# A decoder layer on one core: modulation rows through GpSimd's DMA queue, conditioning row by transposes

## The chip, the core and the metric

One Trainium2 chip, one of its cores. The metric is the device time of one execution in microseconds (us), 1265.94 us as the median of 3 runs of the kernel before (1265.94 to 1266.82). The engines have the profile's names: PE (matmul) with PEld (its weight loads), DVE (vector), ACT (scalar), POOL (GpSimd), SP (which here only issues DMAs). Each engine works through its own instructions in the order in which they stand; semaphores make one wait for another.

## The reference, cut to what matters

One residual layer on x of 256 x 2048 in float32, with a conditioning vector c of 2048:

```
mod = silu(c) @ w_mod + b_mod            # 2048 x 12288, six sections of 2048
sh1, sc1, g1, sh2, sc2, g2 = split(mod, 6)
u = x * (1 + sc1) + sh1
y = token_mixer(u)                       # u @ w_in, then mLSTM heads and HGRN2 heads, then @ w_out
x = layer_norm(alpha * x + (1 + g1) * y)
u = x * (1 + sc2) + sh2
y = (silu(u @ w_gate) * (u @ w_up)) @ w_down     # 5632 wide
x = layer_norm(alpha * x + (1 + g2) * y)
```

HGRN2 has a lower bound `lb`, computed from 8 columns of logits.

## The kernel before, in words

**Modulation.** `w_mod` lies in 96 rows of [128, 2048] floats, 1024 KB each (`in_wmod`). `mod(j)` (line 171) loads row j into a tile `m` of a pool with two buffers (`mr`), and one DVE instruction (L174) multiplies it with `cb` and sums along the row, which gives column j of `modc`. `cb` is silu(c) on all 128 partitions. It is loaded as a broadcast (L140) and put through Silu by ACT. Rows 0 to 15 are the shift and 16 to 31 the scale of the first modulation; they are needed in pairs, one pair for each block k of 128 features (k from 0 to 15). The other 64 rows serve the gate of the first residual, the second modulation and the last gate.

**Activations.** `make_u(k)` (L268) makes block k of u from a slice of `xT` and the pair of columns: one ACT instruction for `t`, one for its rounded part `uh`, one DVE subtraction for the rest, `ul`. `xT` comes in four loads of four blocks each.

**Weights.** All other weights come as tiles of [128, 1024] floats, 512 KB (`wr`, four buffers). ACT rounds each into `wh` (five buffers), DVE subtracts to get the rest `wl` (five buffers, L213 in the first stages and L715 later), and PE runs three matmuls for each product: high by high, low by high, high by low. So each weight tile costs one ACT instruction, one DVE instruction and 24 matmuls of 256 columns or their like.

**Stages.** First stage: the input projection, in an order written in `STAGES`: sections q and f for blocks 0 to 3, then the other sections for blocks 0 to 7, then q and f for blocks 4 to 15. `prep` calls `mod(16+k)`, `mod(k)` and `make_u(k)` for each block as it is due. Then the rest of the projection with the HGRN2 and mLSTM work between its tiles; then the output projection (`wo`) with the mLSTM tail and the first layer norm; then the feed-forward part, nearly two thirds of the time. Further mod rows are called at set rates between tiles (`mods_some`, L610ff.), and the last ones in the feed-forward part (`some` at L787, called at L906, and `up_to`).

**Order.** The order of the code is not the order on the engines. A scheduler walks through the instructions by priority and by when it thinks their inputs and buffers are ready, and fixes one order for each engine. The loads of mod rows and of weight tiles are all issued by SP, in that one order: an issue that waits for a free buffer holds up all that stand behind it. The lower bound's Exp needs another function table on ACT.

Of the kernel before, what the change touches and what calls it, by code (L numbers as in the profile page):

```python
# [3 lines left out]
F32 = mybir.dt.float32  # L4
F32R = mybir.dt.float32r
U8 = mybir.dt.uint8
AF = mybir.ActivationFunctionType
ALU = mybir.AluOpType

P = 128  # L10
# [69 lines left out]
def build(nc, tc, d):  # L80
    from contextlib import ExitStack

    with ExitStack() as ctx:
# [41 lines left out]
        def act(out, in_, f, **kw):  # L125
            if f in sets:
                use_set(f)
            i = nc.scalar.activation(out, in_, f, **kw).ins  # L128
            if f in sets:
                tc.add_manual_dep(i, table["load"].name, order, reason="table")  # L130
                table["used"].append(i)
            return i
# [4 lines left out]
        mm = nc.tensor.matmul  # L137

        cb = cst.tile([P, D], F32, name="cb")
        nc.sync.dma_start(cb, d["c"].broadcast_to([P, D]))  # L140
        pk = cst.tile([P, NPK], F32, name="pk")
        nc.sync.dma_start(pk, d["pk"])
        kc = cst.tile([P, NCST], F32, name="kc")
        kr = cst.tile([P, 256], F32R, name="kr")
        mk = cst.tile([P, NMK], U8, name="mk")

# [10 lines left out]
        one = cst.tile([P, P], F32, name="one1")  # L157
        nc.gpsimd.memset(one, 1.0)

        for i in range(2):  # L160
            o = cb[:, 1024 * i : 1024 * i + 1024]
            act(o, o, AF.Silu)
        init = cst.tile([P, 96], F32, name="init")
        nc.vector.tensor_copy(init, pc("bmod", 0, 96))
        for s in (1, 2, 4, 5):
            ts(init[:, 16 * s : 16 * s + 16], pc("bmod", 16 * s, 16), 1.0, None, ALU.add)
        ca = cst.tile([P, 16], F32, name="ca")
        act(ca, pc("c", 0, 16), AF.Silu)
        modc = cst.tile([P, 96], F32, name="modc")

        def mod(j):
            t = mr.tile([P, D], F32, tag="m", name=f"m{j}")
            nc.sync.dma_start(t, d["wmod"][j])
            table["mod"] = nc.vector.tensor_tensor_reduce(t, t, cb, 1.0, init[:, j : j + 1], ALU.mult, ALU.add, modc[:, j : j + 1]).ins  # L174
            yield

# [92 lines left out]
        def make_u(k):  # L269
            u = S(T, "t", bufs=CFG["t"])  # L270
            if k % 4 == 0:
                xt["t"] = M(name="xT")
                nc.sync.dma_start(xt["t"], d["x"][k // 4])
            act(u, xt["t"][:, (k % 4) * T : (k % 4) * T + T], AF.Identity, scale=col(1, k), bias=col(0, k))
            split(kt(uh, k), kt(ul, k), u)

# [24 lines left out]

        def lower_bound():
            e, pr = lbt[:, 0:8], lbt[:, 8:16]
            tt(e, pc("lb", 0, 8), pc("lb", 0, 8), ALU.subtract)
            act(e, e, AF.Exp)
            nc.vector.reciprocal(pr, e)
            tt(pr, pr, e, ALU.mult)
            tt(lb, pr, pr, ALU.subtract)
            ts(oml, lb, -1.0, 1.0, ALU.mult, ALU.add)
# [14 lines left out]
        def fq_part(k0, k1):  # L324
            banks = [ps() for _ in range(8)]
            for k in range(k0, k1):
                prep(k + 1)
                if k == 3:
                    nc.sync.dma_start(kc, d["kc"])
                    mf = M(NMK, name="mf")  # L330
                    nc.sync.dma_start(mf, d["mk"])
                    nc.vector.tensor_copy(mk, mf)
                    act(kr[:, 0:P], ident, AF.Copy)
                    act(kr[:, P:], kc[:, 192:320], AF.Copy)
                for c, (h, l) in enumerate(next_win()):
                    gB(banks[4 * c : 4 * c + 4], h, l, 1, 1024, uh, ul, k, k == k0, k == k1 - 1)
                    yield
            if k1 == KT:
                next(ga)
            for i in range(8):  # L340
                evac(k0, "fq", i, banks[i])
# [649 lines left out]
def lay(x, c, w_mod, b_mod, w_in, conv_w, conv_b, b_igate, b_fgate, mlstm_norm_w, hgrn_norm_w, lb_logits, w_out, ln1_g, ln1_b, w_gate, w_up, w_down, ln2_g, ln2_b):  # L991
    import numpy as np

    def tile(w, k0, nk, c0, n):
        return w[k0 * P : (k0 + nk) * P, c0 : c0 + n].reshape(nk, P, n).transpose(1, 0, 2).reshape(P, nk * n)

    def cols(v):
        return v.reshape(-1, P).T

    def few(v, at):  # L1000
        return np.concatenate([np.zeros((at, 1), np.float32), v.reshape(-1, 1), np.zeros((P - at - v.size, 1), np.float32)])

    wm, wi, wo, wg, wu, wd = w_mod[0], w_in[0], w_out[0], w_gate[0], w_up[0], w_down[0]
    a = {}
    a["c"] = c.reshape(1, D)
    a["wmod"] = np.ascontiguousarray(wm.T).reshape(96, P, D)
    a["wmk"] = np.concatenate([wm[:, s * D : s * D + D].reshape(KT, P, D) for s in PE_SECT] or [wm[:1, :1].reshape(1, 1, 1)])
    a["x"] = x[0].T.reshape(4, 4, P, T).transpose(0, 2, 1, 3).reshape(4, P, 1024)
    a["pk"] = np.concatenate(
        [cols(b_mod), cols(conv_w), cols(conv_b), cols(mlstm_norm_w), cols(hgrn_norm_w), cols(lb_logits), cols(ln1_g), cols(ln1_b), cols(ln2_g), cols(ln2_b), few(b_igate, 0), few(b_fgate, 32), cols(c)],  # L1010
        axis=1,
    )
    pl = win_plan()
    a["win"] = np.stack([np.concatenate([tile(wi, *p), tile(wi, *q)], axis=1) for p, q in zip(pl[::2], pl[1::2])])
    z = np.zeros((D, 28), np.float32)
    a["wg"] = tile(np.concatenate([wi[:, 3072:3076], z, wi[:, 3076:3080]], axis=1), 0, KT, 0, 36)
    a["wo"] = np.stack([tile(wo, 8 * part + 2 * p, 2, 512 * i, 512) for part in (1, 0) for i in range(4) for p in range(4)])
    a["wf"] = np.stack([np.concatenate([tile(wg, k, 1, 512 * g, 512), tile(wu, k, 1, 512 * g, 512)], axis=1) for g in range(DFF // 512) for k in range(KT)])
    a["wd"] = np.stack([tile(wd, k, 2, 512 * c, 512) for c in range(4) for k in range(0, FB, 2)])
    a["xr"] = x[0].reshape(2, P, D)  # L1020
    for n, v in (("l1g", ln1_g), ("l1b", ln1_b), ("l2g", ln2_g), ("l2b", ln2_b)):
        a[n] = v.reshape(1, D)
    kc = np.zeros((P, NCST), np.float32)
    s = np.arange(P)
    kc[:, 0:128] = np.eye(P)
    kc[:, 128:192] = (s[:, None] % 64) == np.arange(64)[None, :]
    kc[:, 192:320] = np.where(s[:, None] <= s[None, :], 0.0, -1e30)
    a["kc"] = kc
    mk = np.zeros((P, NMK), np.float32)
    for i, cc in enumerate((1, 2, 4, 8, 16, 32)):  # L1030
        ss, t = (s % 64)[:, None], np.arange(64)[None, :]
        mk[:, 64 * i : 64 * i + 64] = (ss // (2 * cc) == t // (2 * cc)) & (ss % (2 * cc) < cc) & (t % (2 * cc) >= cc)
    a["mk"] = mk
    for k in ("win",):
        a[k] = a[k].reshape(-1, P, 2, 1024).transpose(0, 2, 1, 3)
    return {k: np.ascontiguousarray(v) for k, v in a.items()}
# [17 lines left out]
```

## Time and profile before

| | |
|---|---|
| median of the runs | 1265.94 us |
| the profiled execution's own time, and its span | 1265.78 us, 1264.0 us |
| PE / DVE / ACT / POOL busy | 1212.8 / 901.2 / 591.7 / 3.9 us |
| granted TensorE clock, mean | 0.99 of full speed |
| DMA, mean over the span | 260 GB/s |
| mod rows on DVE | 96, 225.1 us busy in total |
| weight tiles on DVE | 408, 360.6 + 135.8 us at the two lines (the page's ACT and DVE rows have them) |

Busy shares are means over stages that differ. The stages below are cut by tiles: at 43 us PE starts on block 3, by 214 us DVE has done 68 weight tiles, by 377 us 111, and the first layer norm's statistics are summed at 508 us. PE's matmuls are pipelined and their ends are modelled, so short waits of PE are seen best as gaps.

### The profile page before, as it was taken

The page shows a single profiled execution, that of the slowest core. Times are in us where ns is not written, and L with a number is a line of the kernel's source. Part 1 is how long each engine was busy: PE and PEld are TensorE (multiplying, and loading weights), DVE is VectorE, ACT ScalarE, POOL GpSimd, SP SyncE. Part 2 cuts the span into 40 slices and gives each one's busy share as a digit, 9 for nine tenths or more (in the row PEclk, how much of TensorE's full clock was granted, in tenths as well). Part 3 has the DMA queues.
Part 4 walks back from the last instruction along what each step waited for, and adds up shares of the span by engine and source line. Part 5 has one row for each costly group of instructions (what it writes and reads, how often), then busy time and mean ns, then how long its engine had stood idle before and what let it go on. Part 6 is the DMA issues. An engine that isn't in the chain of part 4 may idle for free.

```text
span 1264.0 us, 17132 instructions
## 1 busy us (share of the span) xinstructions
PE 1212.8 (96%) x6706; PEld 1040.0 (82%) x6706; DVE 901.2 (71%) x979; ACT 591.7 (47%) x743; POOL 3.9 (0%) x13
## 2 busy tenths in 40 slices
PE   4899999999999999799999999999999999999995
PEld 4888899997889887688888888888888888888884
DVE  6778997999999979997877554455555445445655
ACT  4554454835664644644544444433344444434340
POOL 0000000000000000000000000000000000000000
PEclk9999999999999999899999999999999999999998
DMA  9998997857788989889998666666666666676661
GB/s 364 386 335 328 341 398 285 301 200 264 267 327 308 330 317 334 305 320 327 324 329 325 192 190 189 178 194 191 198 191 192 189 194 185 193 256 184 191 191 66
DMA packets 75968, 328.00 MB, mean 260 GB/s; under 512 B 8432, under 2 KB 8816, under 8 KB 62704
## 3 DMA queue, kind: packets, MB, share of 16 engines
q1 hardware_dynamic: 75888, 326.92, 74.9%
q8 instruction: 52, 0.85, 0.3%
q14 instruction: 28, 0.23, 0.0%
HBM read 324.79 MB, written 2.10 MB: 259 GB/s over the span
## 4 chain that ended last, share of the span: by engine, by line
PE 89%; DVE 5%; ACT 3%; issue 2%; DMA 1%; DVEq 0%; ACTq 0%
PE ps L722 21%; PE ps L725 21%; PE ps L721 21%; PE ps L251 5%; PE ps L249 5%; PE ps L250 5%; PE ps L260 2%; PE ps L261 2%; PE ps L262 2%; DVE m L174 2%; PE ps L447 1%; ACT wh L128 1%; DMA m<-in_wmod 1%; DVE wl L213 1%; PE ps L863 1%
## 5 line engine op out<-in xcount | busy, mean ns | idle before, releaser
L128 ACT ACTIVATE wh<-wr 128x1024 fp32r<-128x1024 f32 x408 | 431.1, 1059 | 550.8 <-PE ps L722 426.2
L715 DVE TENSOR_TENSOR wl<-wr,wh 128x1024 fp32r<-128x1024 f32 x296 | 360.6, 1224 | 283.7 <-ACT wh L128 280.4
L721 PE MATMUL ps<-wh,u2h 128*128 128x512 f32 x704 | 275.6, 392 | 0.3 <-ACT s L128 0.3
L722 PE MATMUL ps<-wh,u2l 128*128 128x512 f32 x704 | 273.7, 389 | 0.1
L174 DVE CUSTOM_DVE_ANT_0 m<-m,cb,init 128x2048 f32<-128x2048 f32 x96 | 225.1, 2346 | 22.3 <-DMA m<-in_wmod 22.0
L725 PE MATMUL ps<-wl,u2h 128*128 128x512 f32 x704 | 217.0, 389 | 0.0
L249 PE MATMUL ps<-uh,wh 128*128 128x256 f32 x640 | 184.4, 292 | 22.5 <-ACT wh L128 17.1
L250 PE MATMUL ps<-ul,wh 128*128 128x256 f32 x640 | 181.8, 286 | 0.0
L251 PE MATMUL ps<-uh,wl 128*128 128x256 f32 x640 | 180.3, 287 | 1.1 <-DVE wl L213 1.0
L721 PEld LDWEIGHTS ps<-wh,u2h 128*128 128x128 f32 x704 | 132.6, 188 | 28.9 <-ACT s L128 0.7
L722 PEld LDWEIGHTS ps<-wh,u2l 128*128 128x128 f32 x704 | 132.0, 188 | 28.0 <-DVE u2l L838 0.8
L725 PEld LDWEIGHTS ps<-wl,u2h 128*128 128x128 f32 x704 | 132.1, 188 | 27.6
L213 DVE TENSOR_TENSOR wl<-wr,wh 128x1024 fp32r<-128x1024 f32 x112 | 135.8, 1221 | 25.1 <-ACT wh L128 24.5
L249 PEld LDWEIGHTS ps<-uh,wh 128*128 128x128 f32 x640 | 123.6, 194 | 25.0 <-ACT wh L128 17.8
L721 PE MATMUL ps<-wh,hid 128*128 128x512 f32 x352 | 137.2, 390 | 0.0
L725 PE MATMUL ps<-wl,hid 128*128 128x512 f32 x352 | 137.0, 389 | 0.0
L722 PE MATMUL ps<-wh,hid 128*128 128x512 f32 x352 | 137.0, 389 | 0.0
L250 PEld LDWEIGHTS ps<-ul,wh 128*128 128x128 f32 x640 | 124.5, 195 | 1.3 <-issue 1.0
L251 PEld LDWEIGHTS ps<-uh,wl 128*128 128x128 f32 x640 | 123.2, 194 | 1.9 <-DVE wl L213 1.8
L725 PEld LDWEIGHTS ps<-wl,hid 128*128 128x128 f32 x352 | 66.1, 188 | 13.9
L721 PEld LDWEIGHTS ps<-wh,hid 128*128 128x128 f32 x352 | 66.1, 188 | 13.6
L722 PEld LDWEIGHTS ps<-wh,hid 128*128 128x128 f32 x352 | 66.1, 188 | 13.6
(179 smaller groups left out, 1017.8 us busy)
## 6 DMA issues: line engine op xcount, KB each, us to landing
m<-in_wmod SPq DMA_DIRECT2D x96, 1024.0 KB, 7.1
wr<-in_wf SPq DMA_DIRECT2D x176, 512.0 KB, 4.2
wr<-in_win SPq DMA_DIRECT2D x112, 512.0 KB, 6.0
wr<-in_wd SPq DMA_DIRECT2D x88, 512.0 KB, 3.6
wr<-in_wo SPq DMA_DIRECT2D x32, 512.0 KB, 5.4
xT<-in_x SPq DMA_DIRECT2D x4, 512.0 KB, 8.0
z<-in_xr SPq DMA_DIRECT2D x2, 1024.0 KB, 8.6
out<-z SPq DMA_DIRECT2D x8, 256.0 KB, 2.4
```

Source lines behind the costliest of these rows:

```text
L128: i = nc.scalar.activation(out, in_, f, **kw).ins
L174: table["mod"] = nc.vector.tensor_tensor_reduce(t, t, cb, 1.0, init[:, j : j + 1], ALU.mult, ALU.add, modc[:, j : j + 1]).ins
L213: tt(l[:, :m], r[:, :m], h[:, :m].bitcast(F32), ALU.subtract)
L249: mm(o, h[:, wsl], kt(uh, k0 + k), start=st, stop=False, skip_group_check=True)
L250: mm(o, h[:, wsl], kt(ul, k0 + k), start=False, stop=False, skip_group_check=True)
L251: mm(o, l[:, wsl], kt(uh, k0 + k), start=False, stop=en, skip_group_check=True)
L260: mm(o, a, h[:, w], start=first and k == 0, stop=False, skip_group_check=True)
L261: mm(o, a, l[:, w], start=False, stop=False, skip_group_check=True)
L715: tt(l, r, h.bitcast(F32), ALU.subtract)
L721: mm(o, a, h[:, w], start=first, stop=False, skip_group_check=True)
L722: mm(o, b, h[:, w], start=False, stop=False, skip_group_check=True)
L725: mm(o, a, l[:, w], start=False, stop=last, skip_group_check=True)
```

## The change

1. `mod(j)` issues its load from GpSimd instead of SP. The 96 loads leave SP's queue and stand in POOL's. The two buffers stay.
2. The broadcast load of c and the two Silu instructions over it are gone. ACT computes silu of the 16 columns of c in `pk`; PE transposes each column, broadcast along 128, into a PSUM bank (16 transposes, 4 banks), and ACT and DVE copy two banks each into `cb`. The identity that transposes need is the first 128 columns of `kc`; they are now loaded near the start, the other 192 later.
3. The first `xT` tile comes in four slices.
4. The remaining constants and the masks (`mf`) are called for at block 5 instead of 3.
5. The lower bound must stand behind a mod instruction on DVE.

```diff
         cb = cst.tile([P, D], F32, name="cb")
-        nc.sync.dma_start(cb, d["c"].broadcast_to([P, D]))
         pk = cst.tile([P, NPK], F32, name="pk")
         nc.sync.dma_start(pk, d["pk"])
         kc = cst.tile([P, NCST], F32, name="kc")
+        nc.sync.dma_start(kc[:, 0:128], d["kc"][:, 0:128])
...
-        for i in range(2):
-            o = cb[:, 1024 * i : 1024 * i + 1024]
-            act(o, o, AF.Silu)
+        ca = cst.tile([P, 16], F32, name="ca")
+        act(ca, pc("c", 0, 16), AF.Silu)
+        for b in range(4):
+            o = ps()
+            for j in range(4):
+                nc.tensor.transpose(o[:, P * j : P * j + P], ca[:, 4 * b + j : 4 * b + j + 1].broadcast_to([P, P]), ident)
+            if b % 2:
+                nc.vector.tensor_copy(cb[:, 512 * b : 512 * b + 512], o)
+            else:
+                act(cb[:, 512 * b : 512 * b + 512], o, AF.Copy)
...
             t = mr.tile([P, D], F32, tag="m", name=f"m{j}")
-            nc.sync.dma_start(t, d["wmod"][j])
+            nc.gpsimd.dma_start(t, d["wmod"][j])
...
                 xt["t"] = M(name="xT")
-                nc.sync.dma_start(xt["t"], d["x"][k // 4])
+                if k:
+                    nc.sync.dma_start(xt["t"], d["x"][k // 4])
+            if k < 4:
+                w = slice(k * T, k * T + T)
+                nc.sync.dma_start(xt["t"][:, w], d["x"][0][:, w])
...
-            tt(e, pc("lb", 0, 8), pc("lb", 0, 8), ALU.subtract)
+            i = tt(e, pc("lb", 0, 8), pc("lb", 0, 8), ALU.subtract).ins
+            tc.add_manual_dep(i, table["mod"].name, order, reason="late")
...
-                if k == 3:
-                    nc.sync.dma_start(kc, d["kc"])
+                if k == 5:
+                    nc.sync.dma_start(kc[:, 128:], d["kc"][:, 128:])
```

The scheduler makes another order of it on every engine. Three places:

DVE at the start, before (`m` is a mod row, `wl` the low part of a weight tile, `ul` that of a block of u, `lbt` the lower bound):

```order
L164 COPY init<-pk 128x96
L304 TENSOR_TENSOR lbt_119<-pk 128x8
L166 TENSOR_SCALAR init<-pk 128x16 x4
L306 RECIPROCAL lbt_119<-lbt_119 128x8
L174 ISA m_128,modc<-m_128,cb,init 128x2048
...
L174 ISA m_131,modc<-m_131,cb,init 128x2048
L174 ISA modc 128x1
L231 TENSOR_TENSOR ul_111<-t_134,uh_109 128x256
L213 TENSOR_TENSOR wl_143<-wr_140,wh_142 128x1024
L213 TENSOR_TENSOR wl_173<-wr_170,wh_172 128x1024
```

The first two mod rows stand behind each other here, with the rest of the lower bound between them.

DVE at the same place now (four banks are copied to `cb` first, two of them by ACT):

```order
L167 COPY cb<-ps_106 128x512
L167 COPY cb<-ps_118 128x512
L179 ISA m_150,modc<-m_150,cb,init 128x2048
L179 ISA modc 128x1
L218 TENSOR_TENSOR wl_165<-wr_162,wh_164 128x1024
L218 TENSOR_TENSOR wl_195<-wr_192,wh_194 128x1024
L218 TENSOR_TENSOR wl_236<-wr_233,wh_235 128x1024
L218 TENSOR_TENSOR wl_266<-wr_263,wh_265 128x1024
L179 ISA m_153,modc<-m_153,cb,init 128x2048
L179 ISA modc 128x1
L218 TENSOR_TENSOR wl_307<-wr_304,wh_306 128x1024
L236 TENSOR_TENSOR ul_133<-t_156,uh_131 128x256
```

The second mod row, which completes the first pair, stood right behind the first; now four weight tiles stand between them.

SP at the start, before (`wr` is a weight tile, 512 KB):

```order
L140 DMA cb<-in_c 128x2048
L142 DMA pk<-in_pk 128x242
L173 DMA m_128<-in_wmod 128x2048
L173 DMA m_131<-in_wmod 128x2048
L273 DMA xT_135<-in_x 128x1024
L208 DMA wr_140<-in_win 128x1024
L208 DMA wr_170<-in_win 128x1024
L173 DMA m_200<-in_wmod 128x2048
L173 DMA m_203<-in_wmod 128x2048
L208 DMA wr_210<-in_win 128x1024
```

Mod rows and weight tiles stand in one queue, two and two.

SP now, its first five issues, and a stretch from the sixteenth on (`wg` are the gate weights):

```order
L141 DMA pk<-in_pk 128x242
L143 DMA kc<-in_kc 128x128
L282 DMA xT_157<-in_x 128x256
L213 DMA wr_162<-in_win 128x1024
L213 DMA wr_192<-in_win 128x1024
...
L213 DMA wr_452<-in_win 128x1024
L279 DMA xT_1105<-in_x 128x1024
L339 DMA kc<-in_kc 128x192
L341 DMA mf_1428<-in_mk 128x384
L279 DMA xT_1657<-in_x 128x1024
L376 DMA wg_2142<-in_wg 128x576
L213 DMA wr_485<-in_win 128x1024
```

SP has no mod row left. Four weight tiles are issued before anything waits, and the later x tiles, constants, masks and gate weights stand ahead of the tenth weight tile; POOL issues the mod rows, each behind the DVE instruction that frees its buffer.

DVE in the output projection, before (`sc` are columns of the second modulation):

```order
L174 ISA m_4723,modc<-m_4723,cb,init 128x2048
L174 ISA modc 128x1
L715 TENSOR_TENSOR wl_4517<-wr_4514,wh_4516 128x1024
L794 TENSOR_TENSOR sc<-pk,modc 128x4
L795 TENSOR_TENSOR sc<-pk,modc 128x4
L796 TENSOR_TENSOR sc<-sc,modc 128x4
L715 TENSOR_TENSOR wl_4538<-wr_4535,wh_4537 128x1024
L715 TENSOR_TENSOR wl_4556<-wr_4553,wh_4555 128x1024
L715 TENSOR_TENSOR wl_4577<-wr_4574,wh_4576 128x1024
L715 TENSOR_TENSOR wl_4595<-wr_4592,wh_4594 128x1024
L715 TENSOR_TENSOR wl_4616<-wr_4613,wh_4615 128x1024
L174 ISA m_4770,modc<-m_4770,cb,init 128x2048
```

One mod row stands for six tiles in this stretch.

DVE in the output projection now, at about the same tile:

```order
L725 TENSOR_TENSOR wl_4522<-wr_4519,wh_4521 128x1024
L179 ISA m_5361,modc<-m_5361,cb,init 128x2048
L179 ISA modc 128x1
L725 TENSOR_TENSOR wl_4542<-wr_4539,wh_4541 128x1024
L725 TENSOR_TENSOR wl_4563<-wr_4560,wh_4562 128x1024
L179 ISA m_5364,modc<-m_5364,cb,init 128x2048
L179 ISA modc 128x1
L725 TENSOR_TENSOR wl_4581<-wr_4578,wh_4580 128x1024
L179 ISA m_5403,modc<-m_5403,cb,init 128x2048
L179 ISA modc 128x1
L725 TENSOR_TENSOR wl_4602<-wr_4599,wh_4601 128x1024
L725 TENSOR_TENSOR wl_4620<-wr_4617,wh_4619 128x1024
```

Mod rows stand closer together here; rows that the code calls for later, in the feed-forward part, stand in this stage now. Counted over the whole of DVE's order, the mod rows that stand ahead of a given place are:

| place in DVE's order | before | now |
|---|---|---|
| ahead of the 7th weight tile | 8 | 5 |
| ahead of the 68th | 32 | 43 |
| ahead of the 111th | 54 | 65 |
| ahead of the first layer norm's BN_AGGR | 70 | 86 |

## Rows read from the trace of the kernel before

**Rows 1.** The page: span, busy us by engine, chain that ended last

```profile
span 1264.0 us, 17132 instructions
...
PE 1212.8 (96%) x6706; PEld 1040.0 (82%) x6706; DVE 901.2 (71%) x979; ACT 591.7 (47%) x743; POOL 3.9 (0%) x13
...
PE 89%; DVE 5%; ACT 3%; issue 2%; DMA 1%; DVEq 0%; ACTq 0%
```

**Rows 2.** Windows by stage: stretch, length, busy us (count) by engine, clock, DMA

```profile
0.00:43.00 43.00, 21.02 (x147) 20.45 (x148) 29.08 (x37) 17.89 (x25) 2.38 (x11) 1.00 0.95 373
43.00:214.00 171.00, 168.05 (x1204) 158.43 (x1203) 143.16 (x142) 87.90 (x112) 1.48 (x2) 0.99 0.90 344
214.00:377.00 163.00, 158.85 (x1392) 142.02 (x1390) 155.69 (x208) 99.34 (x166) 0.00 (x0) 0.99 0.76 272
377.00:507.00 130.00, 127.11 (x666) 108.47 (x664) 116.66 (x138) 64.83 (x83) 0.00 (x0) 1.00 0.90 323
507.00:1264.00 757.00, 737.72 (x3304) 610.59 (x3304) 456.60 (x458) 321.75 (x361) 0.00 (x0) 0.99 0.68 220
```

**Rows 3.** Windows, one stretch of the feed-forward part

```profile
800.00:900.00 100.00, 100.00 (x443) 82.81 (x442) 52.57 (x49) 38.77 (x37) 0.00 (x0) 1.00 0.64 193
```

**Rows 4.** Timeline of PE: start, length, what, count, [idle before <-releaser]

```profile
16.66 0.58 PE L249 MATMUL ps<-uh,wh 128*128 128x256 f32 x1 [16.66 <-ACT wh L128]
...
42.65 0.74 PE L249 MATMUL ps<-uh,wh 128*128 128x256 f32 x4 [3.78 <-ACT uh L128]
...
512.28 3.67 PE L817 MATMUL ps<-kc,z 128*128 128x128 f32 x16 [8.17 <-DVE z L810]
```

**Rows 5.** Timeline of DVE, the mod rows at L174 of the first 40 us

```profile
9.47 2.35 DVE L174 CUSTOM_DVE_ANT_0 m<-m,cb,init 128x2048 f32<-128x2048 f32 x1
...
12.22 2.35 DVE L174 CUSTOM_DVE_ANT_0 m<-m,cb,init 128x2048 f32<-128x2048 f32 x1
...
21.20 2.35 DVE L174 CUSTOM_DVE_ANT_0 m<-m,cb,init 128x2048 f32<-128x2048 f32 x1
...
29.27 2.35 DVE L174 CUSTOM_DVE_ANT_0 m<-m,cb,init 128x2048 f32<-128x2048 f32 x1
...
38.36 2.35 DVE L174 CUSTOM_DVE_ANT_0 m<-m,cb,init 128x2048 f32<-128x2048 f32 x1 [0.20 <-DMA m<-in_wmod]
```

**Rows 6.** Everything on tile m: landing times of its 96 loads

```profile
DMA to landing us min/median/max: 4.8/7.1/9.9
```

**Rows 7.** The chain of waits, first step: start us, us, what

```profile
0.74 4.77 DMA cb<-in_c
```

**Rows 8.** Windows, DMA near full: last come DMA share, GB/s

```profile
3.00:14.00 11.00, 0.00 (x0) 0.00 (x0) 5.32 (x13) 4.88 (x6) 0.00 (x0) 1.00 1.01 408
```

**Rows 9.** DMA issues: KB of one, median us from issue to landing

```profile
pk<-in_pk SPq DMA_DIRECT2D x1, 121.0 KB, 5.1
```

**Rows 10.** The page, costliest groups: rounding and subtraction of a weight tile

```profile
L128 ACT ACTIVATE wh<-wr 128x1024 fp32r<-128x1024 f32 x408 | 431.1, 1059 | 550.8 <-PE ps L722 426.2
...
L213 DVE TENSOR_TENSOR wl<-wr,wh 128x1024 fp32r<-128x1024 f32 x112 | 135.8, 1221 | 25.1 <-ACT wh L128 24.5
```

**Rows 11.** Timeline of ACT: block 0 of u

```profile
14.61 0.60 ACT L128 ACTIVATE t<-xT,modc 128x256 f32<-128x256 f32 x1 [4.16 <-DVE modc L174]
15.24 0.42 ACT L128 ACTIVATE uh<-t 128x256 fp32r<-128x256 f32 x1
```

**Rows 12.** Windows by stage, tile m alone: DVE busy us (mod rows)

```profile
0.00:43.00 43.00, 18.73 (x8) 1.00 0.95 373
43.00:214.00 171.00, 56.32 (x24) 0.99 0.90 344
```

**Rows 13.** Waits of DVE, 43 to 214 us: us in total, times, longest

```profile
DVE wl L213 <- ACT wh L128: 17.9, 20, 2.9
```

**Rows 14.** Waits of SP, the whole span

```profile
SPq L173 <- DVE modc L174: 133.4, 44, 6.0
```

More of the change, by code (lines that the diff above doesn't have):

```diff
@@ L166, in build @@
             ts(init[:, 16 * s : 16 * s + 16], pc("bmod", 16 * s, 16), 1.0, None, ALU.add)
-        ca = cst.tile([P, 16], F32, name="ca")
-        act(ca, pc("c", 0, 16), AF.Silu)
         modc = cst.tile([P, 96], F32, name="modc")
@@ L1004, in lay @@
     a = {}
-    a["c"] = c.reshape(1, D)
     a["wmod"] = np.ascontiguousarray(wm.T).reshape(96, P, D)
```

## The prediction

> **What bounds the kernel now.** I read the page's head first, then the busy time in five stages, then the first 46 us of each engine in order of time, and last the waits of SP and DVE. The page says PE: 1212.8 of 1264.0 us, and 89% of the chain that ended last [rows 1]. The stages say more [rows 2]. In the feed-forward part PE is full in every stretch with DVE half idle [rows 3]. From 43 to 507 us PE is nearly full too (454 of 464 us), but DVE is close behind it: 143.16 of 171, 155.69 of 163, 116.66 of 130 us, 415.5 of 464 in all, and the DMA engines are at a share of 0.90 in the first and last of these. Only in the first 43 us does PE wait for long: it starts at 16.66 us and gets block 3 of u at 42.65 us [rows 4]. So there are two places where a change can move the end: the arrival of the first four blocks, and DVE (or DMA) becoming the limit between 43 and 507 us. What leaves DVE after 507 us is worth nothing.
>
> The first 43 us are a chain of mod rows. The second, fourth, sixth and eighth start on DVE at 12.22, 21.20, 29.27 and 38.36 us [rows 5]; they share one of the two buffers, so each waits for a load that could be issued only when the one before it was done. From the end of the second (12.22 + 2.35 = 14.57) to the end of the eighth (40.71) are three turns of 8.7 us: 2.35 us of DVE and about 6.3 us of issue to landing, a little under the median of 7.1 [rows 6].
>
> **The change part by part.** *Broadcast load, Silu, lower bound.* The load of c took 4.77 us, two Silu 2.00 us [rows 7]. With 1.05 MB (1024 KB) at 408 GB/s [rows 8] taking 2.6 us, 2.2 us of the 4.77 are fixed. In their place come 16 transposes, 3.67 us for the 16 of the trace [rows 4], twice that if the clock is at its lower level then, and two copies behind each other. `pk` now leads the queue: it lands between 3.3 us (0.74 + 2.2 + 0.3) and 5.9 us (its own 5.1, [rows 9]), so `cb` stands between 7.8 and 14 us. The first mod row began at 9.47; it now begins between 9 and 14. This is not what ends the wait, as the next step shows, so I cost it at nothing; at the late end it costs 4 us.
>
> *The second mod row behind four weight tiles.* On DVE four tiles stand between the first and the second mod row now. The fourth must land first. Ahead of it, in whichever order, go two mod rows (2.10 MB), four tiles (2.10), two slices of x, `pk` and the identity (0.45): 4.65 MB, 11.4 us at 408 GB/s. From the first issue at 0.74, with 2.2 us fixed, that is 14.3 us; ACT's rounding 1.06 and DVE's subtraction 1.22 [rows 10] make it 16.6, and the second mod row ends at 19.0 instead of 14.57. After it t and uh (0.60 + 0.42, [rows 11]): PE starts at about 20.1 instead of 16.66.
>
> *The turns.* From there the chain is as before, three turns through one buffer, each a landing and 2.35 us plus 0.05: the eighth mod row ends at 19.0 + 3 x (L + 2.4). In the old queue a mod load had the DMA engines for itself as far as SP's order let it. Now SP issues tiles as their buffers come free, and four x, constant and gate loads of 2.1 MB besides, while POOL issues mod rows, and both run on the same engines. No row shows two queues side by side, so I take L from the shortest, median and longest landing [rows 6]: 4.8, 7.1, 9.9 give 40.6, 47.5 and 55.9 us against 40.71. I take 7.1, the median: the traffic is about that of the busy stretches where it was measured. Then block 3 arrives at 42.65 + 7 = 49.5 us. **First term: +7 us, from 0 to +15.**
>
> The Trainium skill ("DMA: Bandwidth & Descriptors", Issuing engines are not separate DMA queues) says that DMAs issued by different engines run on the same 16 DMA engines and interleave, and that this saves only issue time. The trace agrees as far as one queue can: from 3 to 14 us SP's queue alone has the share at 1.01 [rows 8]. By this rule the second queue brings no bandwidth, and a mod load beside tiles is slower than alone, the upper part of the range.
>
> *Mod rows drawn forward, 43 to 214 us.* By the 68th tile DVE did 8 + 24 mod rows [rows 12]; now 43 stand there, 11 more, 11 x 2.35 = 25.9 us on an engine that had 171 - 143.16 = 27.8 us free in the stage. DMA carries 58.8 MB there at 344 GB/s; 11 rows add 11.5 MB, and what was loaded ahead (about five tiles, three x tiles, the gate weights) takes off 4.5: 65.8 MB, which needs 385 GB/s to fit into 171 us, against 408 at best. Of DVE's free time 17.9 us were waits for ACT's rounded tile [rows 13], which do not go away because DVE has more to do. If all 25.9 us fit into the gaps it costs nothing; if DMA stays at 344 GB/s the stage takes 191 us, +20. Three engines at 98% of one stage do not fit without friction: I take about 40% of the waits that were there, **second term: +8 us, from 0 to +20.**
>
> *214 to 377 us.* 22 mod rows between the 68th and the 111th tile before and now: 0.
>
> *377 to 507 us.* Five more mod rows up to the layer norm (16 before the change, 21 now): 11.8 us on DVE, which was free for 13.3 us [rows 2]. All of it hidden is 0, none is +12. PE has five buffers of tiles to bridge a mod row of 2.35 us, which hides most of one: **third term: +4 us, from 0 to +12.** Around the layer norm the order is one mod row and the same norm steps, so 0.
>
> *After 507 us* DVE is rid of 16 rows, 37.6 us, beside a PE that is full: 0. That is the price of all this: work moves from a place where it was free to one where it is not. *POOL's issues* are off every engine that counts (POOL busy 3.9 us of the span, [rows 1]); what they may cost is a rival below.
>
> **Sum:** 1264.0 + 7 + 8 + 4 = 1283.0 us of span, and 1.8 us around it as now (1265.78), 1284.8; the profiled execution is 0.2 us below the runs' median. Forecast 1285 us. The three ranges together reach from 1266 to 1313.
>
> **The rivals.**
>
> *The extra rows are absorbed.* DVE's gaps before 507 us sum to 13.9 + 27.8 + 7.3 + 13.3 = 62 us [rows 2], and 16 rows need 37.6. If mod rows fill just the gaps that PE's pace leaves, only the start costs: 1266 + 7 = 1273. For it: in the stage up to 214 us DVE's waits came from PE's pace, not its own. Against it: its order is fixed, so a mod row stands between tiles also when a tile is urgent.
>
> *Faster: SP's queue freed.* SP stood 133.4 us before mod loads whose buffer was still in use, 44 times, with tile loads behind them [rows 14]. If that was what made PE wait, the gaps of PE from 43 to 507 us (3.0 + 4.1 + 2.9 = 10 us) go, and if mod loads win against tiles (L at 4.8 or less) the start costs at most 3: 1266 - 7 = 1259. It decides from the point where block 3 arrives by 46 us. Against it: five tiles wait in buffers between SP and PE, and the gaps of PE lie mostly in HGRN2's own steps, which do not wait for loads.
>
> *Mod loads from POOL land late.* A row through one of two buffers has two periods less its own 2.4 us to land. With 35 rows in 171 us the period is 4.9, so 7.4 us are allowed. With a landing of 9 instead of 7.1, DVE waits (9 - 7.4) / 2 for each of 35 rows, 28 us in place of the 8 of the second term less what overlaps, some 16 more, and the start grows by 3 x 1.9: 1285 + 22 = 1307. For it: every mod load now passes an engine whose DMAs this trace does not show, and the median of 7.1 is near the edge already.
>
> The Trainium skill ("SBUF - State Buffer", Who interferes with whom) says that GpSimd writes descriptors through SBUF ports that it shares with DVE, so that some DVE instructions, those in a two-port mode, hold back a DMA issued by GpSimd until they end, and that tensor_tensor did not. No run here shows it yet. If the tile subtractions or the mod rows themselves held it back, each load would come later by up to one of them, 1.22 or 2.35 us, which is this rival.
>
> **How the numbers follow.** Forecast as summed 0.48 (1275 to 1300), absorbed 0.20 (1273), late landings 0.15 (1307), faster 0.12 (1259), and 0.05 that it ends within 0.2% (2.5 us, what a measurement of this kernel can tell from no change). Faster 0.12, same 0.05, slower 0.83. The range from 1264 to 1310 leaves out most of the faster case and the end of the late one.
>
> **What would show it.** Right: the second mod row starts on DVE at 16 to 18 us, behind four tiles; PE starts near 20 and has block 3 near 50 us; DVE is over 97% busy up to the 68th tile, reached 10 to 20 us later; the layer norm's PE gap near 527 us; the feed-forward part as long as before. Wrong in the first term: mod loads land in 5 us beside tiles. Wrong in the second: the 68th tile at 214 + 7. The forecast falls altogether if block 3 comes before 43 us, or if the feed-forward part itself changes in length.

## The result and the profile after: slower by 4.3%

The changed kernel takes 1319.14 us (1316.91 to 1325.78, four runs), the kernel before 1265.94 in the same comparison: ratio 1.043, 95% interval 1.0406 to 1.0455. Forecast were 1285 us and 1264 to 1310. The direction was right, the loss is 53 us and not 19. The profiled execution took 1321.25 us, 2.1 above the median.

From the page of the changed kernel: the span, busy us (share, count) by engine, the chain that ended last by engine.

```profile
span 1319.5 us, 17219 instructions
...
PE 1225.7 (93%) x6722; PEld 1048.7 (79%) x6722; DVE 901.1 (68%) x981; ACT 589.5 (45%) x743; POOL 55.0 (4%) x109
...
PE 62%; issue 22%; DMA 7%; DVE 6%; POOL 2%; ACT 0%; SPq 0%; DVEq 0%; POOLq 0%; ACTq 0%
```

DVE has the same work to 0.1 us [rows 1]. PE's share of the chain falls from 89% to 62%, but much of the chain's "issue" lies beside a PE that is full (from 285.78 to 334.43 us, for one), so the loss is read from stages instead. The stages of [rows 2] can't be compared directly: its cuts at 214 and 377 us are the ends of the 67th and the 109th weight tile, not of the 68th and the 111th, which end at 218.3 and 385.7 us. So here are both kernels, cut at the same places of the program: PE's start on block 3 of u, DVE's end of the 67th and of the 111th weight tile, the first layer norm's statistics. The columns are the stretch, its length, busy us and count of PE, PEld, DVE, ACT and POOL, the granted clock, DMA share and GB/s. The changed kernel:

```profile
0.00:53.39 53.39, 25.68 (x160) 24.86 (x160) 33.80 (x38) 19.86 (x26) 6.14 (x18) 0.78 0.94 358
53.39:246.90 193.51, 172.25 (x1208) 161.19 (x1209) 162.57 (x166) 83.67 (x109) 18.80 (x36) 0.96 0.92 345
246.90:429.40 182.50, 171.17 (x1474) 152.76 (x1472) 163.85 (x220) 106.20 (x174) 14.44 (x26) 0.98 0.72 252
429.40:564.90 135.50, 119.86 (x578) 99.41 (x578) 121.38 (x148) 58.69 (x74) 11.11 (x21) 0.95 0.91 347
564.90:1319.50 754.60, 736.72 (x3304) 610.50 (x3304) 419.46 (x417) 321.08 (x361) 4.47 (x8) 0.99 0.63 196
```

The kernel before:

```profile
0.00:42.65 42.65, 20.67 (x144) 20.10 (x144) 28.73 (x37) 17.54 (x25) 2.38 (x11) 1.00 0.95 373
42.65:214.20 171.55, 168.60 (x1205) 158.97 (x1206) 143.71 (x143) 88.45 (x112) 1.48 (x2) 0.99 0.90 344
214.20:385.70 171.50, 167.35 (x1451) 149.54 (x1450) 164.09 (x218) 104.50 (x173) 0.00 (x0) 0.99 0.76 272
385.70:508.70 123.00, 118.42 (x606) 100.75 (x604) 109.76 (x132) 59.47 (x74) 0.00 (x0) 0.99 0.90 327
508.70:1264.00 755.30, 737.72 (x3304) 610.59 (x3304) 454.90 (x455) 321.75 (x361) 0.00 (x0) 0.99 0.68 220
```

The five stages are longer by 10.7, 22.0, 11.0, 12.5 and -0.7 us, which sums to the 55.5 us of the spans. In the second stage the DMA share and rate are nearly those of before, so it moves 66.8 MB instead of 59.0 at about the same rate. PE idles 42.6 us more in all, and its own busy time is 12.9 us longer (1225.7 for 1212.8) at a mean granted clock of 0.971 for 0.989; no run here parts that from the idle time.

The second stage for tile m alone (columns: DVE, POOL, clock, share, GB/s):

```profile
53.40:246.90 193.50, 82.20 (x35) 18.51 (x35) 0.96 0.92 345
```

So the three stages from block 3 to the norm have 35, 22 and 21 rows in DVE's order, where the kernel before has 24, 22 and 16. In the third stage the count is the same, but the rows are bunched more: 17 of the 22 stand behind at least 91 weight tiles, 14 before. Narrower windows of the changed kernel show it (all engines):

```profile
300.00:340.00 40.00, 40.00 (x420) 33.96 (x420) 39.44 (x63) 24.27 (x44) 0.54 (x1) 1.00 0.48 155
340.00:390.00 50.00, 50.00 (x293) 43.64 (x291) 40.90 (x51) 26.91 (x53) 4.77 (x9) 1.00 0.87 316
390.00:435.00 45.00, 33.55 (x201) 29.10 (x201) 37.64 (x45) 17.50 (x27) 4.22 (x8) 0.86 0.81 293
```

From 300 to 340 us, with two rows, the DMA engines are half idle; of the next 95 us, with 19 rows, PE loses 11.5, all of it behind 390 us. Waits of the changed kernel (us in total, times, longest), DVE's first:

```profile
DVE m L179 <- DMA m<-in_wmod: 62.4, 37, 3.6
DVE wl L218 <- ACT wh L128: 9.9, 10, 2.5
```

```profile
PE ps L254 <- ACT uh L128: 24.4, 4, 16.3
...
PE gps L384 <- DVE q L299: 9.3, 1, 9.3
PE ps L599 <- DVE s L593: 8.0, 1, 8.0
```

Before, DVE waited 24.5 us in these tiles for ACT's rounding [rows 10] and 22.0 us for mod rows; now it waits mostly for mod rows. One way in which that reaches PE stands in DVE's timeline before the 9.3 us wait, which ends at 245.34 us:

```profile
236.30 1.22 DVE L218 TENSOR_TENSOR wl<-wr,wh 128x1024 fp32r<-128x1024 f32 x1
241.09 2.35 DVE L179 CUSTOM_DVE_ANT_0 m<-m,cb,init 128x2048 f32<-128x2048 f32 x1 [3.57 <-DMA m<-in_wmod]
...
243.37 1.22 DVE L218 TENSOR_TENSOR wl<-wr,wh 128x1024 fp32r<-128x1024 f32 x1
244.51 1.28 DVE L299 TENSOR_TENSOR q<-ps,q 128x512 f32<-128x512 f32 x2
```

A row of a later stage waits 3.57 us for its load, and the evacuation of the bank that PE needs (`q`) stands behind it. How much of the loss goes this way is a question for the runs.

### The profile page after: what moved, and what is told of

It reads as the page before. It is cut to its first block, busy times and chain, and to the rows that moved or that the text cites. A ratio compares the mean times of both kernels' runs of the same rounds, so it can differ in the third digit from the quotient of the medians.

```text
span 1319.5 us, 17219 instructions
## 1 busy us (share of the span) xinstructions
PE 1225.7 (93%) x6722; PEld 1048.7 (79%) x6722; DVE 901.1 (68%) x981; ACT 589.5 (45%) x743; POOL 55.0 (4%) x109
## 4 chain that ended last, share of the span: by engine, by line
PE 62%; issue 22%; DMA 7%; DVE 6%; POOL 2%; ACT 0%; SPq 0%; DVEq 0%; POOLq 0%; ACTq 0%
PE ps L731 19%; PE ps L732 19%; PE ps L735 19%; DMA wr<-in_win 3%; DMA m<-in_wmod 2%; POOL m L178 1%; DVE m L179 1%; DVE wl L218 1%; DVE wl L725 1%; PE ps L873 1%; DMA mf<-in_mk 1%; PE ps L254 1%; PE ps L255 1%; PE ps L256 1%; DMA wr<-in_wo 1%
## 5 line engine op out<-in xcount | busy, mean ns | idle before, releaser
L179 DVE CUSTOM_DVE_ANT_0 m<-m,cb,init 128x2048 f32<-128x2048 f32 x96 | 225.2, 2347 | 62.7 <-DMA m<-in_wmod 62.4
L254 PE MATMUL ps<-uh,wh 128*128 128x256 f32 x640 | 187.4, 298 | 29.3 <-ACT uh L128 24.4
L256 PE MATMUL ps<-uh,wl 128*128 128x256 f32 x640 | 185.2, 290 | 4.8 <-DVE wl L218 4.8
L255 PE MATMUL ps<-ul,wh 128*128 128x256 f32 x640 | 185.1, 290 | 0.3 <-DVE ul L236 0.3
L256 PEld LDWEIGHTS ps<-uh,wl 128*128 128x128 f32 x640 | 127.0, 198 | 5.8 <-DVE wl L218 5.8
L255 PEld LDWEIGHTS ps<-ul,wh 128*128 128x128 f32 x640 | 127.4, 199 | 2.2 <-issue 1.2
```

The source lines that it names most:

```text
L254: mm(o, h[:, wsl], kt(uh, k0 + k), start=st, stop=False, skip_group_check=True)
L255: mm(o, h[:, wsl], kt(ul, k0 + k), start=False, stop=False, skip_group_check=True)
L256: mm(o, l[:, wsl], kt(uh, k0 + k), start=False, stop=en, skip_group_check=True)
```

## The experiments

Theory 1: the order of DVE that comes with POOL's queue (mod rows drawn forward) makes the time. Theory 2: the queue itself does. Theory 3: the other edits do. Later theory 1 was divided: what a row drawn forward costs is DVE's time (V), its transfer (T), or a wait for one of two buffers that holds up what is queued behind it (W). All medians, with the ratio to the kernel before on the same chip; "67 tiles" is when DVE's timeline ends the 67th weight tile, "rows" DVE's waits for mod rows. "Old order" has as many mod rows ahead of each weight tile as the kernel before, "new order" as the changed one (pool_alone differs from it in four of the 96 rows). The four quarter versions leave out three quarters of each row's data or of its sum, so their times serve for differences alone.

| run | queue | order | us | ratio, 95% | 67 tiles | rows |
|---|---|---|---|---|---|---|
| before | SP | old | 1265.94 | | 214.2 | 22.0 |
| changed | POOL | new | 1319.14 | 1.0406-1.0455 | 246.9 | 62.4 |
| sp_again | SP | old | 1270.28 | 1.0021-1.0045 | 216.8 | 28.3 |
| late_parts | SP | old | 1269.25 | 1.0021-1.0048 | 219.7 | 20.7 |
| pool_alone | POOL | new | 1318.91 | 1.0382-1.0440 | 243.7 | 60.3 |
| pool_old_order | POOL | old | 1279.84 | 1.0074-1.0123 | 217.0 | 15.6 |
| pool_old_start | POOL | old | 1279.65 | 1.0093-1.0122 | 219.9 | 22.9 |
| sp_new_order | SP | new | 1349.39 | 1.0631-1.0666 | 264.4 | 73.4 |
| quarter_load_new | POOL | new | 1261.54 | 0.9955-0.9979 | 211.0 | 5.8 |
| quarter_load_old | POOL | old | 1253.05 | 0.9888-0.9917 | 204.5 | 0.9 |
| quarter_reduce_new | POOL | new | 1298.45 | 1.0241-1.0276 | 234.6 | 122.5 |
| quarter_reduce_old | POOL | old | 1256.56 | 0.9915-0.9945 | 213.2 | 21.8 |
| new_three_buffers | POOL | new | 1325.12 | 1.0450-1.0485 | 246.4 | 0.4 |
| new_two_buffers | POOL | new | 1352.88 | 1.0674-1.0709 | 262.1 | 51.8 |
| old_three_buffers | POOL | old | 1282.38 | 1.0110-1.0143 | 219.0 | 2.6 |
| old_two_buffers | POOL | old | 1291.49 | 1.0188-1.0226 | 218.9 | 20.2 |
| rows_later | SP | later | 1299.21 | 1.0251-1.0282 | 213.3 | 32.0 |

### Queue, order and the other edits

The changed kernel with one part undone (sp_again), and the kernel before with one part done (pool_alone), differ from their originals in this line:

```diff
-            nc.gpsimd.dma_start(t, d["wmod"][j])
+            nc.sync.dma_start(t, d["wmod"][j])
```

> The changed kernel with the modulation rows on SP's queue again; the transposes, the sliced constants, the sliced first x tile and the late lower bound stay. Its VectorE order has as many modulation rows ahead of each weight tile as the kernel before (32 ahead of the 68th, 70 ahead of the norm). Theory 1 (the order that comes with the POOL queue makes the time): 1260 to 1270 us, block 3 starting at 41 to 45 us. Theory 2 (the queue itself makes it): the same 1260 to 1270. Theory 3 (the other edits, at the start, make it): above 1300.

> The kernel before with nothing changed but the queue of the modulation rows (POOL's): the 1 MB broadcast of the conditioning row, the whole constants and the early lower bound are back. Its order has 43 rows ahead of the 68th tile and 86 ahead of the norm, as the changed kernel's. Theories 1 and 2: 1310 to 1325 us, nearly the whole loss. Theory 3: 1262 to 1275.

pool_alone is the changed kernel to 0.2 us: the queue's line brings the loss. Theory 3 falls, except for the 4 us of sp_again. To part the queue from its order, order-only dependencies pin the rows between the tiles (AHEAD[j] tiles stand ahead of row j; the numbers below are those of the old order). They make nobody wait for another engine. They hold the rows' places among the weight tiles and nothing else; the scheduler still arranges the rest of each engine's order anew:

```diff
+AHEAD = (0, 0, 2, 2, 4, 4, 6, 6, 9, 10, 13, 15, 18, 19, 23, 24,
...
+            mrow.append(table["mod"])
...
-                    tt(l[:, :m], r[:, :m], h[:, :m].bitcast(F32), ALU.subtract)
+                    wlow.append(tt(l[:, :m], r[:, :m], h[:, :m].bitcast(F32), ALU.subtract).ins)
...
+        for j, n in enumerate(AHEAD):
+            if n:
+                tc.add_manual_dep(mrow[j], wlow[n - 1].name, order, reason="behind")
+            tc.add_manual_dep(wlow[n], mrow[j].name, order, reason="ahead")
```

> The changed kernel, POOL's queue included, with order-only dependencies that give VectorE the number of modulation rows ahead of every weight tile that the kernel before has. Theory 1 (order): 1262 to 1278 us, VectorE's waits for modulation rows in the stages after block 3 back near the 22 us of before. Theory 2 (the queue itself: rows that share the DMA engines with the weights and land late): 1300 to 1320, with 50 us or more of such waits left.

> The kernel before, all loads on SP's queue, with order-only dependencies that give VectorE the number of modulation rows ahead of every weight tile that the changed kernel has (43 ahead of the 68th, 86 ahead of the norm). Theory 1 (order): 1300 to 1340 us with the old queue, as long or longer than the changed kernel, TensorE short of work in the same two stretches (225 to 250 and 400 to 425 us). Theory 2 (queue): 1270 to 1290, the VectorE work that is drawn forward and no more.

Theory 1 holds in the main: with the queue kept and the order put back, 39.3 of the 53.2 us go (1319.14 - 1279.84), though 1279.84 is 2 us above the range that I gave for it. With SP's queue kept and the order changed the kernel loses 83.1 us (1349.39 - 1266.26), above the 1340 expected, so the new order is worse on the old queue. There tile loads stand behind loads of rows, for which SP waits 179 us (133.4 before, [rows 14]); that this is the reason was not tested alone. Next, the queue's own price at the old start (the pinned order on the kernel before, with POOL's queue):

> The kernel before with the rows on POOL's queue and VectorE's order held as it was: the queue by itself. With the changed start that step cost 9.6 us (1270.3 to 1279.8). If the queue has a price of its own: 1272 to 1280 us. If those 9.6 us came of the new start's loads meeting the rows: 1264 to 1270.

1279.65 - 1265.73 = 13.9 us, about the same as with the new start: moving the rows to POOL's queue costs something even with the rows in their old places. Its windows up to the norm, cut at the same places as above:

```profile
0.00:48.90 48.90, 22.54 (x145) 21.80 (x145) 29.77 (x38) 20.77 (x27) 6.13 (x18) 0.93 0.96 380
48.90:219.90 171.00, 166.09 (x1197) 158.17 (x1197) 141.53 (x142) 83.76 (x108) 12.98 (x25) 0.99 0.91 338
219.90:392.90 173.00, 170.05 (x1486) 152.70 (x1484) 163.43 (x216) 105.68 (x174) 14.43 (x26) 1.00 0.72 260
392.90:523.60 130.70, 117.77 (x578) 99.09 (x578) 109.96 (x134) 58.48 (x74) 8.47 (x16) 0.97 0.86 322
```

The start is 6.2 us longer than before (48.9 for 42.65) and the stage up to the norm 7.7 (130.7 for 123.0); the two between them differ by -0.5 and 1.5. At the start SP issues the constants at 4.2 us (32.0 before) and three x tiles at 19.1 (45.4 to 155.2 before), ahead of weight tiles, so the scheduler's new order of SP is a rival to the queue there. In the output projection weight tiles land later, this run first and the kernel before second (KB, median us from issue to landing):

```profile
wr<-in_wo SPq DMA_DIRECT2D x32, 512.0 KB, 7.4
```

```profile
wr<-in_wo SPq DMA_DIRECT2D x32, 512.0 KB, 5.4
```

That fits a queue that no longer lets the next tile go ahead of the next row, but no run changed that alone, and none parts the queue from the orders that came with it. For the 4 us of sp_again three small edits were put on the kernel before:

```diff
-                nc.sync.dma_start(xt["t"], d["x"][k // 4])
+                if k:
+                    nc.sync.dma_start(xt["t"], d["x"][k // 4])
+            if k < 4:
+                w = slice(k * T, k * T + T)
+                nc.sync.dma_start(xt["t"][:, w], d["x"][0][:, w])
...
+            tc.add_manual_dep(i, table["mod"].name, order, reason="late")
...
-                if k == 3:
+                if k == 5:
```

> The kernel before with three of the small edits: the first x tile in four slices, the constants and masks at the sixth k step, the lower bound behind the rows; no transposes, all on SP's queue. If the transposes cost the 4 us of the run with SP's queue again: 1262 to 1267 us, and a little faster than before if the later constants help. If the small edits cost them: 1268 to 1272.

1269.25: the small edits cost 3.5 us, and the transposes 1 or nothing. Which of the three it is was not parted. With POOL's queue they cost nothing (1279.84 and 1279.65).

### What a row drawn forward costs

Here both orders are pinned and run with the same edit; the difference is the price of the order. First, a quarter of each load with DVE's work as long as it was:

```diff
-            nc.gpsimd.dma_start(t, d["wmod"][j])
-            table["mod"] = nc.vector.tensor_tensor_reduce(t, t, cb, 1.0, init[:, j : j + 1], ALU.mult, ALU.add, modc[:, j : j + 1]).ins
+            nc.gpsimd.dma_start(t[:, :512], d["wmod"][j][:, :512])
+            table["mod"] = nc.vector.tensor_tensor_reduce(t, cb, cb, 1.0, init[:, j : j + 1], ALU.mult, ALU.add, modc[:, j : j + 1]).ins
```

> The changed kernel in its own order (held by order-only dependencies), but of each modulation row only a quarter is loaded (256 KB, not 1 MB), and the reduction multiplies the conditioning row with itself: as long as before on VectorE, behind the same load, without the row's values. Read against the same edit in the old order; with whole rows the new order cost 39 us over the old one. Theory V (the order costs VectorE's time: 2.35 us for each row drawn forward): the difference stays at 25 to 40. Theory T (the order costs transfers: 1 MB for each row drawn forward, in stretches whose DMA share is above 0.9): it falls to 0 to 12. Theory W (rows stand in VectorE's order more densely than two buffers are filled again, and weight tiles and evacuations wait behind them): 0 to 12 as well, with VectorE's waits for rows near nothing.

> The same quarter loads in the order of the kernel before. All theories: 1235 to 1275 us; what counts is the difference to the run with the new order.

Second, whole loads and a quarter of DVE's work:

```diff
-            table["mod"] = nc.vector.tensor_tensor_reduce(t, t, cb, 1.0, init[:, j : j + 1], ALU.mult, ALU.add, modc[:, j : j + 1]).ins
+            table["mod"] = nc.vector.tensor_tensor_reduce(t[:, :512], t[:, :512], cb[:, :512], 1.0, init[:, j : j + 1], ALU.mult, ALU.add, modc[:, j : j + 1]).ins
```

> The changed kernel in its own order (held), rows loaded whole, but VectorE reduces only the first 512 of their 2048 columns (about 0.6 us instead of 2.35); the other columns are left out of the sums. Read against the same edit in the old order. Theory V: the difference between the orders falls from 39 us to 0 to 12. Theories T and W: it stays at 25 to 40; T with a DMA share above 0.9 and VectorE's waits mostly for weights, W with 40 us or more of VectorE's waits for modulation rows and a DMA share not above that of the old order.

> The same short reductions in the order of the kernel before. All theories: 1255 to 1280 us.

With quarter loads the order costs 8.5 us (1261.54 - 1253.05), with quarter reductions 41.9 (1298.45 - 1256.56), 2 us above the 25 to 40 of T and W. Theory V falls. Of the 8.5 us 7.9 are there when PE starts on block 3 (46.56 us for 38.66): that is the first pair of rows behind four tiles, as in the prediction's first term. Behind block 3 the order costs next to nothing with a quarter of the bytes. Windows up to the 67th tile, quarter loads and then quarter reductions, both in the new order:

```profile
34.00:211.00 177.00, 174.15 (x1274) 165.81 (x1273) 171.90 (x176) 90.48 (x117) 20.73 (x39) 1.00 0.73 235
```

```profile
35.00:235.00 200.00, 182.22 (x1284) 172.18 (x1283) 115.85 (x178) 91.19 (x118) 20.49 (x39) 0.95 0.96 368
```

In the first DVE is busy for 97% of the stretch and PE runs at its pace all the same. In the second DVE is busy for 58%, the DMA share is 0.96, and PE is short of work. That is what T expects; W expected a share no higher than in the old order (0.93), but 122.5 us of waits for rows as well. So these runs don't part T and W. Three buffers were to do that; four of each half of the split weights instead of five make room:

```diff
-CFG = dict(big=10, med=10, wr=4, mr=2, wh=5, wl=5, s5=4, t=3, cm=2)
+CFG = dict(big=10, med=10, wr=4, mr=3, wh=4, wl=4, s5=4, t=3, cm=2)
```

> The changed kernel in its own order (held) with three buffers for modulation rows, and four instead of five for each half of the split weights to make room. Read against the next run, which has the same four and two row buffers. Theory T (the loads drawn forward take the DMA engines' time): less than 8 us between them, the rate to the 68th tile as it was (345 GB/s). Theory W (two buffers filled too slowly for the order): 20 to 40 us faster than the next run, with VectorE's waits for rows down from about 60 us to under 20.

> Control for three buffers: the changed kernel in its own order with two row buffers and four instead of five buffers for each half of the split weights. All theories: 1318 to 1330 us.

> Three row buffers and four of each half of the split weights, POOL's queue, in the order of the kernel before (held). With the new order these buffers gave 1325.1 us, with no waits of VectorE for rows. Theory T: the order keeps most of its price without the waits, so 1285 to 1300 us here. Theory W: it loses its price with them, so 1310 to 1325.

> The control: two row buffers and four of each half of the split weights, POOL's queue, old order. With the new order these buffers gave 1352.9 us. Theory T: 30 to 40 us below that (1313 to 1323). Theory W: 50 us or more below it (1303 at most).

With three buffers hardly anything waits for rows any more (0.4 and 2.6 us), and the order still costs 42.7 us (1325.12 - 1282.38): most of the price is not W's. Of it 11.4 us stand when PE starts on block 3 (62.78 us for 51.37). The second stage, from there to the 67th tile, new order and old order:

```profile
62.80:246.40 183.60, 179.47 (x1283) 169.38 (x1284) 166.24 (x170) 91.42 (x117) 18.83 (x36) 0.98 0.94 365
```

```profile
51.40:219.00 167.60, 167.60 (x1226) 159.93 (x1227) 142.99 (x150) 88.99 (x113) 12.99 (x25) 1.00 0.91 342
```

It is 16 us longer. With two buffers and five of each weight half (the changed kernel and pool_old_order) it is 24 us longer, 193.5 for 169.5. So with a third buffer the rate does rise, from 345 GB/s in the changed kernel to 365, and 16 us of the stage's price are left with next to no waits for rows: T, with a part of W in the changed kernel. The two stages up to the norm add 11 and 7 us more. With four weight buffers and two for rows the order costs 61.4 us (1352.88 - 1291.49), 18.7 more than with three; three row buffers beside five of each weight half were not run, so W's part of the changed kernel's 39 us is not known. The expectations fared worse than the theory: new_two_buffers is 23 us above its range, old_three_buffers 3 below the one of T, and the steps from two to three buffers in the new order (27.8 us) and from new to old order with two buffers (61.4) both lie where I had put W. I had not reckoned with what a weight buffer less costs, nor with T and W at once.

Last, the other direction on the kernel before: the rows from the 49th to the 84th six tiles later (their AHEAD raised by 6).

> The kernel before, all on SP's queue, with the modulation rows from the 49th to the 84th put six weight tiles later in VectorE's order (64 rows ahead of the norm, not 70). Theory T: a row costs about 3 us of transfer ahead of the norm and nothing in the feed-forward: 1248 to 1262 us, faster than both kernels. If the rows are then late for the second normalised input, or only take their place behind the norm: 1264 to 1280.

1299.21 us, above both ranges. The edit did less than it was meant to: the norm is not tied to weight tiles, and 68 rows stand ahead of it, not 64 (70 before). Sixteen rows stand between the 67th and the 111th tile (22 before), and 20 between there and the norm (16 before). Windows of these two stages, cut as above:

```profile
213.30:384.90 171.60, 167.46 (x1451) 149.69 (x1450) 153.00 (x210) 104.81 (x173) 0.00 (x0) 0.99 0.68 242
384.90:523.00 138.10, 123.80 (x606) 102.44 (x604) 115.72 (x136) 59.52 (x74) 0.00 (x0) 0.96 0.86 311
```

Six rows less where the share was 0.76 save nothing (171.6 for 171.5 us). Four rows more where it was 0.90 come with 15.1 us more (138.1 for 123.0); their 4.2 MB would be 13 us at the 327 GB/s of before. The rest of the loss, some 20 us, lies behind the norm, and there the expectation's other case is seen: rows of the second modulation come late. The last columns `sc`, which DVE computes from 562.7 us on before, it computes from 611.7 here, and PE waits for the part of the second normalised input that needs them:

```profile
615.92 0.80 PE L724 MATMUL ps<-wh,u2h 128*128 128x512 f32 x1 [3.95 <-ACT u2h L130]
```

So a row is nearly free at a share of 0.76 and dear at 0.9 ahead of the norm; behind it, transfers and lateness were not parted. No version that computes the whole layer beat the kernel before: its PE is busy for 286 of the 293 us from 214 to 507 [rows 2].

## Why the prediction fell short

The direction was right, the size was not: 1319 us lies above the range. **The step that failed is the price of rows drawn forward**, in the second and in the third term: their bytes were taken to fit beside the rest because DVE had time free, so most of their cost was called hidden. The two terms add 12 us in the prediction and 34.5 in the trace. A stage between them that was put at nothing adds 11 more. The runs show that a row drawn into a busy stage costs its transfer: with a quarter of its bytes the order's price behind block 3 is next to nothing, with a third of its DVE time the price stays.

**The view of the bounds** was right in part: the DMA engines at 0.90 in the second and fourth stage, DVE close behind PE. What was wrong is which of the two a row drawn forward meets. The sign given for the second term was DVE over 97% busy up to the 68th tile; it was busy for 84% up to the 67th (162.57 of 193.51 us), no more than before (143.71 of 171.55), with the DMA share at 0.92.

**First term (+7, from 0 to +15): right in kind, +10.7.** The mod rows of the first 53 us on DVE, and PE's two marks:

```profile
7.56 2.35 DVE L179 CUSTOM_DVE_ANT_0 m<-m,cb,init 128x2048 f32<-128x2048 f32 x1 [0.18 <-DVE cb L167]
...
18.35 1.23 DVE L218 TENSOR_TENSOR wl<-wr,wh 128x1024 fp32r<-128x1024 f32 x1 [1.92 <-ACT wh L128]
19.49 2.35 DVE L179 CUSTOM_DVE_ANT_0 m<-m,cb,init 128x2048 f32<-128x2048 f32 x1
...
28.21 2.35 DVE L179 CUSTOM_DVE_ANT_0 m<-m,cb,init 128x2048 f32<-128x2048 f32 x1 [2.55 <-DMA m<-in_wmod]
...
49.90 2.35 DVE L179 CUSTOM_DVE_ANT_0 m<-m,cb,init 128x2048 f32<-128x2048 f32 x1 [2.24 <-DMA m<-in_wmod]
```

```profile
22.98 0.80 PE L254 MATMUL ps<-uh,wh 128*128 128x256 f32 x2 [16.34 <-ACT uh L128]
...
53.39 1.20 PE L254 MATMUL ps<-uh,wh 128*128 128x256 f32 x6 [2.60 <-ACT uh L128]
```

The first row starts at 7.56 us, ahead of the 9 to 14 forecast, which changes nothing, as the prediction had it. The second row waits behind the fourth tile, as forecast, and starts at 19.49 us instead of 16 to 18; PE starts at 22.98 (20.1 forecast). Three turns from 19.49 to 49.90 are 10.1 us each (9.5 forecast). Block 3 comes at 53.39 against 49.5, within the range.

**Second term (+8, from 0 to +20): the step fails here first, +22.0.** I had worked out that the stage would take 191 us if the DMA engines stayed at 344 GB/s, and then took "about 40% of the waits that were there", a share of DVE's free time, which supposed that the rate could rise to 385. It stayed at 345, and the stage took 193.5 us. The 408 GB/s of [rows 8] were eleven microseconds of loads that waited for nothing. Over a whole second stage the most that a kernel with whole rows and whole reductions held was 365, with a third row buffer.

**From the 67th to the 111th tile (0): failed, +11.0.** The count of rows was right (22 and 22), but a count says nothing of where they stand: more of them stand in the last third of the stage, where the DMA share is above 0.8 and PE loses its time. What else enters these 11 us was not parted.

**Third term (+4, from 0 to +12): the same step, +12.5.** The stage took 135.5 us for 123.0, at 0.91 and 347 GB/s. DVE had 13 us free for five more rows, as the prediction said; their 5.2 MB alone are 15 us at that rate (an estimate from the two numbers). With the cuts of [rows 2] the stage would look 5 us longer and the term right; its cut at 377 us lies 9 us short of the 111th tile.

**After the norm (0): right**, 754.6 for 755.3; the 16 rows that left it gave nothing back.

**The rivals.** *Late landings* named a time near the result (1307) for a wrong reason. Everything on tile m after:

```profile
DMA to landing us min/median/max: 5.0/6.8/9.8
```

The median is 6.8 us and was 7.1 [rows 6], so the loads do not land later. DVE's waits for rows nearly tripled (22.0 to 62.4 us) because rows stand densely for two buffers; with a third they vanish, and most of the order's price does not. By the rule of the Trainium skill ("SBUF — State Buffer", Who interferes with whom) a DMA issued by GpSimd could be held back by DVE instructions of a two-port mode. Nothing here shows it: POOL's 96 issues of rows took 0.53 to 0.77 us each, none as long as a tile subtraction (1.22 us) or a reduction (2.35 us), and with reductions of 0.75 us the loads land no sooner (median 8.2). *Absorbed* and *faster* fell with the second stage. "SP's queue freed" may be why the new order costs 83 us on SP's queue and 39 on POOL's, but then it only softens what the order costs. The rule of the Trainium skill that the prediction cites from "DMA: Bandwidth & Descriptors" (Issuing engines are not separate DMA queues), by which a second queue brings no bandwidth, is borne out in the second stage: 344 GB/s with one queue, 345 with two.

## What to carry to other kernels

Where a stage shows a DMA share of 0.9, price a load that is drawn into it by its bytes at the rate that the stage already shows, whatever free time the engine has that consumes it: by that rule the second stage takes 191 us, and 193.5 were measured. Compare stages between the same tiles, not between round times: a cut 9 us off would make one failed term look right. A change of queue can change the order of another engine: count what stands ahead of each place, and look at how densely, not only at totals. Before a wait is blamed, take it away in both orders: three buffers removed nearly all waits for rows and left most of the price.

## What the runs showed of the hardware

Each of the 96 loads occupies POOL for 0.54 us. From the page of pool_old_order (busy us, mean ns):

```profile
L180 POOL DMA_DIRECT2D m<-in_wmod x96 | 51.4, 536 | 628.0 <-DVE modc L181 620.7
```

With the rows on POOL's queue and in their old places (pool_old_start) the rows gain next to nothing, 7.0 us from issue to landing for 7.1, while the weight tiles of the output projection take 7.4 us for 5.4, and the kernel is 13.9 us slower. The rate that the DMA engines held beside computing engines, over a second stage with whole rows, was 330 to 349 GB/s at shares of 0.89 to 0.93 with two row buffers and five of each weight half.
